# Hybrid decoder layer: products on half of TensorE's array padded to the whole or put in pairs, attention values two blocks at a time

## The chip, the cores and the metric

The kernel runs on one core of a Trainium2 chip. The metric is device time in microseconds for one execution. A core has TensorE (matmuls, into PSUM), VectorE (DVE), ScalarE (ACT), GpSimd (POOL) and SyncE (SP), whose queue issues the DMAs. Each engine works through its own instructions in order and waits for others by semaphores.

## The reference, cut to what matters

One layer with two branches, for 1024 prompt tokens and 64 sample tokens (8 sequences of 8), model width 1024, all in fp32:

```python
proj = rmsnorm(h, norm_mix) @ w_in          # 7440 columns, cut into the parts below
# branch A: gated delta rule, 8 heads of 128, chunks; state S per head and sequence
v_new = u_c - w_c @ S
o_c   = (q_c * exp(g)) @ S + (q k^T * decay) @ v_new
S     = S * exp(g_last) + (k_c * exp(g_last - g)).T @ v_new
# branch B: sliding-window attention, 16 query heads of 64 over 4 key heads, window 128, ALiBi, sinks
p = softmax([s, sink]);  o = p @ v          # the sample tokens see 128 cached keys and their own 8
h = h + (sigmoid(ga) * o_a + sigmoid(gb) * o_b) @ w_out
h = h + relu(rmsnorm(h) @ w_up)**2 @ w_down
h = h + sigmoid(rmsnorm(h) @ w_ple_gate) * (p_l @ w_ple_proj)
```

Outputs are the new hidden rows and the caches: last rows before the convolution, delta-rule states, keys and values of the window.

## The kernel before

Activations lie feature-major: 128 features on the partitions, 1088 tokens (1024 prompt, 64 sample) in the free dimension. Every large product is a "gemm": a weight tile of 128 output features is loaded (512 KB), split into a high and a low part (ScalarE copies to `wh`, GpSimd subtracts into `wl`, both double-buffered), and multiplied against the split activations in three matmuls per contraction tile (lines 165 to 167), over token chunks of 384, 384 and 320 columns. After each group of three matmuls, `part` pops one closure from the list `side`; that is how the small work of attention and of the delta rule is put between the gemm matmuls on TensorE's queue. The small products use plain fp32, which TensorE runs as two passes.

The stages, by the time in the profiled execution:
- Up to 54 us: input norms and the projection of the per-layer embedding.
- 54 to 217 us, keys: for each of 8 heads a gemm tile, the convolution, then `key_rows` and `key_products`, which form k k^T per chunk of 128 tokens (line 587) and for the 64 sample tokens a 64-column product (line 599).
- 217 to 435 us: the triangular solves on VectorE (lines 657, 658), in parallel with gemm tiles for the attention's queries, keys and values. `swa_keys` loads the keys of a key head from DRAM into the buffer `kraw` of its own pool and splits them into `khi` and `klo`; `swa_queries` does so for queries, with one difference per half on GpSimd (line 892).
- Up to 640 us, attention: 8 gemm tiles (gates) with 192 side steps. `attend` runs over n = 0 to 65, three steps for each n: `scores(n)` (lines 921, 922, then VectorE adds the bias and takes the maximum, ScalarE the exponential, line 931), `spread(n-1)` (transposes of the weights, line 944, and one ScalarE copy to `pTs`, 2 buffers), `values(n-2)` (line 966: for two halves of the window and two heads e a product on 64 columns, written to partitions 64e to 64e+63 of `psn`). In every sixth step from the 45th on `swa_sample` advances, in three steps for each of 8 sequences: scores, transposes, and the values (lines 1041, 1042), which for each key head take one product of 128 rows (the cached values `cv`) and one of 64 rows (the new values `vss`), all to the same 64 columns.
- 640 to 1196 us, heads: `gdn_head` for each of 8 heads does four gemm tiles (q, v, z, gate) with the chunk scan (`scan_steps`, lines 1247 to 1270) and the sample's part (`sample_steps`) as side steps. Before them come the products of line 1126 and, for the 64 sample tokens, line 1130. `sample_steps` forms a residual `rs` (64 rows), solves it (line 1216), forms its contribution to the output (line 1227), and updates the 8 states in two blocks of 4 sequences: the new values are multiplied by a mask that keeps the rows of these four (`vm`, line 1223), and a product on 64 rows and 512 columns follows (line 1232). At the next head's start `close` transposes the outputs, the sample's on 64 rows (line 1295).
- From 1196 us: output projection, MLP and embedding gate, nearly all gemm.

The order of instructions on each engine is made by the framework's scheduler from the program's order and its own time model; the times above are the chip's.

Of the kernel before, what the change touches and what calls it, by code (L numbers as in the profile page):

```python
# [9 lines left out]
F32 = mybir.dt.float32  # L10
# [7 lines left out]
P = 128  # L18
# [5 lines left out]
H = 8  # L24
# [5 lines left out]
NUP = 32  # L30

# [7 lines left out]
def hybrid_layer(ctx: ExitStack, tc: tile.TileContext, d):  # L39
# [313 lines left out]
    def small(name, n, parts=P, **kw):  # L353
        return lp.tile([parts, n], F32, name=name, tag=name, **kw)
# [6 lines left out]
    xts = small("xts", H * NS, NS)  # L361
# [4 lines left out]
    vss = mp.tile([NS, 4, 64], F32, name="vss")  # L366
# [182 lines left out]
    def key_rows(h, kT):  # L549

        dma(kTd[h], kT)
        E = kp.tile([P, T], F32, name="E", tag="E", bufs=1)
        dma(E[:, :NP], gcd[h * 8 : h * 8 + 8].rearrange("c p -> (c p)")[None, :].broadcast_to([P, NP]))
        dma(E[:, NP:T], gcsd[h : h + 1].broadcast_to([P, NS]))
# [54 lines left out]

    todo = []  # L610
    for h in range(H + 2):
        st = conv_steps(8 + h, kp, lambda: kp.tile([P, T], F32, name="kT", tag="kT")) if h < H else feature_steps()
# [89 lines left out]
    def solve_sample():  # L702
# [31 lines left out]
        for b in range(NB):  # L734
            ts(out=xts.rearrange("p (h b i) -> p h b i", b=NB, i=8)[:, :, b], in0=xe, scalar1=bsel[:, b : b + 1],
               scalar2=None, op0=ALU.mult)
# [36 lines left out]
    def swa_v(i, vf):  # L773

        yield
        vt = qp.tile([P, 9, P], F32, name="vt", tag="vt", bufs=1)
        tok_major(vf, vf[:, NP:T], vt, 1.0)
        dma(d["o_vp"][:, i], vt[:, 7])
        dma(d["o_vs"][:, i], vt[:NS, 8])
        dma(vtd[i], vt[:, 0:8].rearrange("p c f -> p (c f)"))  # L780
        nc.gpsimd.tensor_copy(vss[:, 2 * i : 2 * i + 2].rearrange("p k d -> p (k d)"), vt[:NS, 8])
# [154 lines left out]
    def spread(n):  # L936
# [8 lines left out]
        pT = sp.tile([P, 2, 2, P], F32, name="pTs", tag="pTs")  # L945
# [39 lines left out]
    def attend():  # L985

        for n in range(64 + 2):
# [6 lines left out]
            if 0 <= n - 2 < 64:  # L994
                values(n - 2)
            yield

    def swa_sample():
# [6 lines left out]
        ts(out=nskc, in0=skc, scalar1=-1.0, scalar2=None, op0=ALU.mult)  # L1005
        for b in range(NB):
# [10 lines left out]
            pr = sl.tile([P, P + NS], F32, name="prs", tag="prs", bufs=1)  # L1017
            st = sl.tile([P, 8], F32, name="sts", tag="sts", bufs=2)
            nm, su, es = st[:, 0:1], st[:, 1:2], st[:, 2:3]
            rb_ = rqs[:, b : b + 1]  # L1020
            stt(out=pr[:, :P], in0=S[:, :P], scalar=rb_, in1=tc_, op0=ALU.mult, op1=ALU.add)
            stt(out=pr[:, P:], in0=S[:, P : P + NS], scalar=rb_, in1=tn_[:, b], op0=ALU.mult, op1=ALU.add)
            nc.vector.tensor_reduce(out=nm, in_=pr, axis=AX.X, op=ALU.max)
            stt(out=nm, in0=nm, scalar=-1.0, in1=nskc, op0=ALU.mult, op1=ALU.min)
            act(pr, pr, AF.Exp, bias=nm, accum_out=su)
# [3 lines left out]
            ts(out=pr, in0=pr, scalar1=es, scalar2=None, op0=ALU.mult)  # L1029
            yield  # L1030
            pt = pst()
            nc.tensor.transpose(pt[:, 0:P], pr[:, :P], ident)
            nc.tensor.transpose(pt[:NS, P : 2 * P], pr[:, P:], ident)
            pT = sl.tile([P, 2 * P], F32, name="pTsb", tag="pTsb", bufs=1)
            act(pT[:, :P], pt[:, :P], AF.Copy)
            act(pT[:NS, P:], pt[:NS, P : 2 * P], AF.Copy)
# [6 lines left out]
            pv = po[:64, :P].rearrange("p (j e t) -> p e j t", e=2, t=8)  # L1043
            for e in range(2):
                act(obs[e * 64 : e * 64 + 64, :, b * 8 : b * 8 + 8], pv[:, e], AF.Copy)
# [39 lines left out]
    gp = pool(actx, "gp")  # L1085
    mixd = dr.tile([KT, P, T], F32, name="mixd")

    def gdn_head(h, prev):
# [3 lines left out]
        kT = G("gkT", [P, T], 2)  # L1092
        kt = G("gkt", [P, 8, P])
        kts = G("gkts", [NS, P])
        rg = G("rg", [P, T], 2)
# [3 lines left out]
        dma(rg, Ed[h])  # L1099
        dma(kT, kTd[h])  # L1100
# [29 lines left out]
        mm(ps[:NS, :NS], kT[:, NP:T], q[:, NP:T], start=True, stop=True)  # L1130
# [61 lines left out]
        ot = G("ot", [P, 9, P])  # L1192

# [8 lines left out]
        def sample_steps():  # L1202
# [8 lines left out]
            r = gp.tile([NS, P], F32, name="rs", tag="rs")  # L1211
            stt(out=r, in0=pk[:NS, :P], scalar=nres[:, h : h + 1], in1=vt[:NS, 8], op0=ALU.mult, op1=ALU.add)
# [3 lines left out]
            mm(ps[:NS, :P], xts[:, h * NS : h * NS + NS], r, start=True, stop=True)  # L1216
            vn = gp.tile([NS, P], F32, name="vns", tag="vns")
            act(vn, ps[:NS, :P], AF.Copy)
            vms = []
            for hf in range(2):  # L1220
                vm = gp.tile([NS, 4, P], F32, name="vm", tag="vm")
                bs = slice(hf * 4, hf * 4 + 4)
                tt(vm, vn[:, None, :].broadcast_to([NS, 4, P]), bsel[:, bs][:, :, None].broadcast_to([NS, 4, P]), ALU.mult)
                yield
                if hf == 0:
                    ps = pst()
                    mm(ps[:NS, :P], qk[:NS, NP:T], vn, start=True, stop=True)
                    tt(ot[:NS, 8], ps[:NS, :P], ot[:NS, 8], ALU.add)
                    out_norm(ps[:NS, :P], NS, 8)
                    yield  # L1230
                ps = pst()
                mm(ps, kts, vm.rearrange("p b n -> p (b n)"), start=True, stop=True)  # L1232
                sb = s0[:, bs].rearrange("p b n -> p (b n)")
                tt(sb, sb, ps, ALU.add)
# [51 lines left out]
        def close():  # L1286
            for hf in range(2):
# [246 lines left out]
```

## Time and profile before

| | |
|---|---|
| median of 3 runs | 2181.7 us (2180.86 to 2184.86) |
| profiled execution | 2175.17 us, span 2173.4 us |
| TensorE matmuls busy | 2111.1 us (97%) |
| VectorE, ScalarE, GpSimd busy | 1081.9, 796.6, 706.7 us |
| mean granted TensorE clock | 0.986 |
| DMA | 196.62 MB, 27.6% of 16 engines' span |

"Busy" is the time in which at least one instruction of an engine is under way; the ends of matmuls are modelled, and matmuls overlap, so the distance between the starts of two matmuls says more of TensorE's pace than their lengths. The profiled execution is one of the kernel's executions, taken with the hardware profiler.

### The profile page before, as it was taken

The page shows a single profiled execution, that of the slowest core. Times are in us where ns is not written, and L with a number is a line of the kernel's source. Part 1 is how long each engine was busy: PE and PEld are TensorE (multiplying, and loading weights), DVE is VectorE, ACT ScalarE, POOL GpSimd, SP SyncE. Part 2 cuts the span into 40 slices and gives each one's busy share as a digit, 9 for nine tenths or more (in the row PEclk, how much of TensorE's full clock was granted, in tenths as well). Part 3 has the DMA queues.
Part 4 walks back from the last instruction along what each step waited for, and adds up shares of the span by engine and source line. Part 5 has one row for each costly group of instructions (what it writes and reads, how often), then busy time and mean ns, then how long its engine had stood idle before and what let it go on. Part 6 is the DMA issues. An engine that isn't in the chain of part 4 may idle for free.

```text
span 2173.4 us, 33492 instructions
## 1 busy us (share of the span) xinstructions
PE 2111.1 (97%) x13485; PEld 2010.5 (93%) x13485; DVE 1081.9 (50%) x1724; ACT 796.6 (37%) x1951; POOL 706.7 (33%) x616
## 2 busy tenths in 40 slices
PE   7999998899999999999999999999999999999999
PEld 6899998777889999999998999999999999999999
DVE  6454599776644555455545543233332323333654
ACT  6576432576643443343335223122121212212321
POOL 4333355333234444544445321212121221212121
PEclk9999999999999999999999999999999999999999
DMA  6465343432143133222332221111111111111132
GB/s 245 140 202 186 106 154 104 128 118 91 64 139 101 64 98 121 94 73 86 111 112 78 88 89 40 39 49 42 46 49 39 49 39 49 47 42 49 39 125 80
DMA packets 89575, 196.62 MB, mean 90 GB/s; under 512 B 34124, under 2 KB 45260, under 8 KB 89292
## 3 DMA queue, kind: packets, MB, share of 16 engines
q1 hardware_dynamic: 89420, 194.48, 27.6%
q8 instruction: 106, 1.74, 0.3%
q14 instruction: 49, 0.40, 0.1%
HBM read 145.61 MB, written 50.78 MB: 90 GB/s over the span
## 4 chain that ended last, share of the span: by engine, by line
PE 80%; DVE 10%; ACT 4%; issue 3%; DMA 1%; POOL 1%; SPq 0%; DVEq 0%; ACTq 0%; POOLq 0%
PE ps L165 23%; PE ps L167 22%; PE ps L166 22%; DVE fs L657 3%; DVE LT L658 2%; PE psn L966 1%; PE pst L944 1%; PE psc L1252 1%; PE pst L1232 1%; PE psc L921 1%; ACT pst L568 1%; PE psc L1247 1%; PE psc L922 1%; PE pst L1126 1%; PE psn L1264 1%
## 5 line engine op out<-in xcount | busy, mean ns | idle before, releaser
L134 POOL TENSOR_TENSOR wl<-wr,wh 128x1024 fp32r<-128x1024 f32 x140 | 343.7, 2455 | 903.8 <-ACT wh L133 903.8
L165 PE MATMUL ps<-xh,wh 128*128 128x384 f32 (+1 forms) x1800 | 626.5, 348 | 3.0 <-ACT qf L349 1.6
L166 PE MATMUL ps<-xl,wh 128*128 128x384 f32 (+1 forms) x1800 | 597.6, 332 | 0.0
L167 PE MATMUL ps<-xh,wl 128*128 128x384 f32 (+1 forms) x1800 | 594.5, 330 | 0.0
L165 PEld LDWEIGHTS ps<-xh,wh 128*128 128x128 f32 x1800 | 341.2, 190 | 26.2 <-issue 21.0
L133 ACT ACTIVATE wh<-wr 128x1024 fp32r<-128x1024 f32 x143 | 150.8, 1054 | 526.1 <-PE ps L166 444.2
L166 PEld LDWEIGHTS ps<-xl,wh 128*128 128x128 f32 x1800 | 341.7, 190 | 1.6 <-issue 0.7
L167 PEld LDWEIGHTS ps<-xh,wl 128*128 128x128 f32 x1800 | 340.6, 189 | 1.9 <-issue 0.9
L165 PE MATMUL ps<-uh,wh 128*128 128x384 f32 (+1 forms) x768 | 250.7, 326 | 1.2 <-DVE h L1403 1.2
L167 PE MATMUL ps<-uh,wl 128*128 128x384 f32 (+1 forms) x768 | 250.9, 327 | 0.0
L166 PE MATMUL ps<-ul,wh 128*128 128x384 f32 (+1 forms) x768 | 250.6, 326 | 0.0
L1403 DVE TENSOR_TENSOR h<-h,ps 128x384 f32<-128x384 f32 (+1 forms) x192 | 100.6, 531 | 226.3 <-PE ps L167 226.3
L166 PE MATMUL ps<-pl,wh 128*128 128x384 f32 (+1 forms) x600 | 197.5, 329 | 0.0
L165 PE MATMUL ps<-ph,wh 128*128 128x384 f32 (+1 forms) x600 | 197.4, 329 | 0.0
L167 PE MATMUL ps<-ph,wl 128*128 128x384 f32 (+1 forms) x600 | 197.0, 329 | 0.0
L1389 DVE TENSOR_TENSOR ul<-us,uh 128x384 fp32r<-128x384 f32 (+1 forms) x96 | 98.0, 1022 | 115.3 <-ACT uh L1388 115.3
L165 PEld LDWEIGHTS ps<-uh,wh 128*128 128x128 f32 x768 | 144.1, 188 | 2.0 <-DVE h L1403 2.0
L167 PEld LDWEIGHTS ps<-uh,wl 128*128 128x128 f32 x768 | 144.1, 188 | 0.0
L166 PEld LDWEIGHTS ps<-ul,wh 128*128 128x128 f32 x768 | 144.1, 188 | 0.0
L508 DVE SCALAR_TENSOR_TENSOR cacc<-raw,cw,cacc 128x1112 f32<-128x1112 f32 x72 | 109.5, 1521 | 62.0 <-ACT cacc L506 56.7
L1387 ACT ACTIVATE us<-ut 128x384 f32<-128x384 f32 (+1 forms) x96 | 48.2, 502 | 197.6 <-DVE ut L1386 196.1
L1386 DVE SCALAR_TENSOR_TENSOR ut<-ps,rb 128x384 f32<-128x384 f32 (+1 forms) x96 | 51.3, 535 | 138.2 <-PE ps L167 138.2
(407 smaller groups left out, 3472.1 us busy)
## 6 DMA issues: line engine op xcount, KB each, us to landing
wr<-win SPq DMA_DIRECT2D x60, 512.0 KB
wr<-wup SPq DMA_DIRECT2D x32, 512.0 KB
wr<-wdn SPq DMA_DIRECT2D x32, 512.0 KB
ppd<-ppo SPq DMA_DIRECT2D x8, 544.0 KB
kTd<-kT SPq DMA_DIRECT2D x8, 544.0 KB
Ed<-E SPq DMA_DIRECT2D x8, 544.0 KB
rg<-Ed SPq DMA_DIRECT2D x8, 544.0 KB
gkT<-kTd SPq DMA_DIRECT2D x8, 544.0 KB
```

What stands on the lines that cost most here:

```text
L133: act(hv, rv, AF.Copy)
L134: (nc.gpsimd if i > 1 else nc.vector).tensor_tensor(lv, rv, hv.bitcast(F32), ALU.subtract)
L165: mm(ps[:M, :w], a, h[:, c0 : c0 + w], start=(k == 0), stop=False)
L166: mm(ps[:M, :w], a, l[:, c0 : c0 + w], start=False, stop=False)
L167: mm(ps[:M, :w], b, h[:, c0 : c0 + w], start=False, stop=(k == n - 1))
L508: stt(out=cc, in0=raw[:, j : j + CONVW], scalar=cw[:, f, j : j + 1], in1=cc, op0=ALU.mult, op1=ALU.add)
L657: tt(tmp, X[:, j : j + 1, j + 1 :].broadcast_to(sh), X[:, 0:j, j : j + 1].broadcast_to(sh), ALU.mult)
L658: tt(X[:, 0:j, j + 1 :], X[:, 0:j, j + 1 :], tmp, ALU.add)
L1386: stt(out=t, in0=ps[:, :w], scalar=0.0, in1=rb2[:, c0 : c0 + w], op0=ALU.max, op1=ALU.mult)
L1387: act(s, t, AF.Square)
L1389: tt(lo[:, c0 : c0 + w], s, hi[:, c0 : c0 + w].bitcast(F32), ALU.subtract)
L1403: tt(hc, hc, ps[:, :w], ALU.add)
```

## The change

What it does:
- Attention: `values` runs for two blocks in a row in every second step, with four buffers of `pTs`. `kraw` is gone; the keys are loaded into `klo` itself and replaced there by the difference.
- Sample attention: the new values and the transposed weights get rows of zeros up to 128, and the output of key heads of odd number goes to partitions 64 to 127.
- Sample products of the delta rule: the stationary operand is widened from 64 to 72 columns (`MS`) and, where the contraction ran over 64 rows, `rs`, `vns`, `xts` and the decay matrix get zero rows; the transpose of line 1295 takes 128 rows. GpSimd writes the zeros.
- State update: one mask multiplication; each half of the sequences uses the 32 rows that belong to it, both products in one step.

```diff
+MS = 72
...
-    xts = small("xts", H * NS, NS)
+    xts = small("xts", H * NS + MS - NS)
+    nc.gpsimd.memset(xts, 0.0)
...
-    vss = mp.tile([NS, 4, 64], F32, name="vss")
+    vss = mp.tile([P, 4, 64], F32, name="vss")
+    nc.gpsimd.memset(vss[NS:P], 0.0)
...
+        nc.gpsimd.memset(E[NS:P, NP:T], 0.0)
...
-        mm(ps[:NS, :NS], kT[:, NP:T], kT[:, NP:T], start=True, stop=True)
+        mm(ps[:MS, :NS], kT[:, NP : NP + MS], kT[:, NP:T], start=True, stop=True)
...
-        raw = ep.tile([P, NP], F32, name="kraw", tag="kraw", bufs=1)
...
+        raw = lo.bitcast(F32)
...
-        pT = sp.tile([P, 2, 2, P], F32, name="pTs", tag="pTs")
+        pT = sp.tile([P, 2, 2, P], F32, name="pTs", tag="pTs", bufs=4)
...
-            if 0 <= n - 2 < 64:
+            if n % 2 and n > 1:
+                values(n - 3)
                 values(n - 2)
...
-            for kv in range(4):
-                o = slice(kv * 32, kv * 32 + 32)
-                mm(po[:64, o], cv[:, kv], pT[:, o], start=True, stop=False)
-                mm(po[:64, o], vss[:, kv], pT[:NS, P + kv * 32 : P + kv * 32 + 32], start=False, stop=True)
...
+            for i in range(2):
+                for c, v in enumerate((cv, vss)):
+                    for e in range(2):
+                        kv = 2 * i + e
+                        mm(po[e * 64 : e * 64 + 64, i * 32 : i * 32 + 32], v[:, kv], pT[:, c * P + kv * 32 : c * P + kv * 32 + 32],
+                           start=(c == 0), stop=(c == 1))
...
-        kT = G("gkT", [P, T], 2)
+        kT = G("gkT", [P, NP + MS], 2)
+        nc.gpsimd.memset(kT[:, T:], 0.0)
...
-        mm(ps[:NS, :NS], kT[:, NP:T], q[:, NP:T], start=True, stop=True)
+        mm(ps[:MS, :NS], kT[:, NP : NP + MS], q[:, NP:T], start=True, stop=True)
...
-            r = gp.tile([NS, P], F32, name="rs", tag="rs")
+            r = gp.tile([P, P], F32, name="rs", tag="rs")
+            nc.gpsimd.memset(r[NS:P], 0.0)
...
-            mm(ps[:NS, :P], xts[:, h * NS : h * NS + NS], r, start=True, stop=True)
+            mm(ps[:MS, :P], xts[:, h * NS : h * NS + MS], r, start=True, stop=True)
+            vn = gp.tile([P, P], F32, name="vns", tag="vns")
+            nc.gpsimd.memset(vn[NS:P], 0.0)
...
+            tt(vm, vn[:NS, None, :].broadcast_to(sh4), bsel4[:, :, None].broadcast_to(sh4), ALU.mult)
+            yield
+            ps = pst()
+            mm(ps[:MS, :P], qk[:, NP : NP + MS], vn, start=True, stop=True)
...
+            pss = [pst() for _ in range(2)]
+            for hf, ps in enumerate(pss):
+                o = slice(hf * 32, hf * 32 + 32)
+                mm(ps, kts[o], vm[o].rearrange("p b n -> p (b n)"), start=True, stop=True)
...
-                    nc.tensor.transpose(pt[:, :NS], ot[:NS, 8], ident[:NS, :NS])
+                    nc.tensor.transpose(pt[:, :P], ot[:, 8], ident)
```

## Rows read from the trace of the kernel before

**Rows 1.** The page, busy us (share of the span) xinstructions.
```profile
PE 2111.1 (97%) x13485; PEld 2010.5 (93%) x13485; DVE 1081.9 (50%) x1724; ACT 796.6 (37%) x1951; POOL 706.7 (33%) x616
```
**Rows 2.** Stretches: length, busy us of PE, PEld, DVE, ACT, POOL, PEclk, DMA.
```profile
366.00:435.00 69.00, 54.66 (x346) 47.92 (x346) 54.61 (x98) 32.63 (x77) 20.65 (x10) 0.89 0.38 119
435.00:640.00 205.00, 199.83 (x1592) 166.81 (x1589) 130.14 (x303) 126.78 (x377) 62.54 (x39) 0.99 0.31 97
640.00:1196.00 556.00, 545.86 (x3609) 502.97 (x3608) 284.51 (x455) 217.47 (x640) 267.80 (x351) 0.99 0.30 96
```
**Rows 3.** Chain of waits from 435 to 640 us, shares by line.
```profile
by line: PE ps L165 14.3%; PE psn L966 13.9%; PE pst L944 10.8%; PE ps L166 10.5%; PE ps L167 10.3%; PE psc L921 5.3%; PE psc L922 5.1%; DMA gkt<-ktd 4.0%; PE pst L1041 3.6%; PE pst L1042 3.6%; ACT pr L931 2.2%; DVE nm L929 2.1%; DVE pr L92
```
**Rows 4.** TensorE in order of time (start us, us, instruction): whole and half product.
```profile
811.76 0.34 PE L165 MATMUL ps<-xh,wh 128*128 128x384 f32 x1
811.94 0.40 PE L1252 MATMUL psc<-r,xt 128*128 128x128 f32 x2
812.09 0.42 PE L166 MATMUL ps<-xl,wh 128*128 128x384 f32 x1
812.35 0.34 PE L167 MATMUL ps<-xh,wl 128*128 128x384 f32 x1
812.61 0.43 PE L1216 MATMUL pst<-rs,xts 64*64 64x128 f32 x2
812.97 0.44 PE L165 MATMUL ps<-xh,wh 128*128 128x384 f32 x1
813.25 0.34 PE L166 MATMUL ps<-xl,wh 128*128 128x384 f32 x1
```
**Rows 5.** TensorE in order of time, one block of the state update.
```profile
683.29 0.42 PE L167 MATMUL ps<-xh,wl 128*128 128x384 f32 x1
683.64 1.12 PE L1232 MATMUL pst<-vm,gkts 64*128 64x512 f32 x2
684.69 0.44 PE L165 MATMUL ps<-xh,wh 128*128 128x384 f32 x1
```
**Rows 6.** TensorE in order of time, one block of attention values.
```profile
515.82 0.31 PE L167 MATMUL ps<-xh,wl 128*128 128x320 f32 x1
516.06 0.66 PE L966 MATMUL psn<-pTs,vt 128*64 128x128 f32 x8
516.64 0.42 PE L165 MATMUL ps<-xh,wh 128*128 128x320 f32 x1
516.90 0.31 PE L166 MATMUL ps<-xl,wh 128*128 128x320 f32 x1
```
**Rows 7.** TensorE in order of time, first and last of a sample block's values.
```profile
603.88 0.30 PE L1041 MATMUL pst<-pTsb,cv 128*64 128x32 f32 x2
...
605.72 0.41 PE L165 MATMUL ps<-xh,wh 128*128 128x320 f32 x1
```
**Rows 8.** TensorE in order of time, a 64-column product behind whole ones.
```profile
1001.02 1.95 PE L1126 MATMUL pst<-q,gkT 128*128 128x128 f32 x16
1002.89 0.33 PE L1130 MATMUL pst<-q,gkT 128*64 128x64 f32 x2
1003.15 0.66 PE L1139 MATMUL psn<-cst,q 128*128 128x128 f32 x4
```
**Rows 9.** Waits from 435 to 640 us: total us, times, longest.
```profile
PEld pst L944 <- ACT pr L931: 5.3, 13, 0.8
```
**Rows 10.** GpSimd and VectorE in order of time, second key head's operands.
```profile
417.31 5.69 POOL L892 TENSOR_TENSOR qst<-qraw,qst 64x1024 fp32r<-64x1024 f32 x2 [4.42 <-ACT qst L891]
419.38 1.42 DVE L879 TENSOR_TENSOR klo<-kraw,khi 128x1024 fp32r<-128x1024 f32 x1 [5.69 <-ACT khi L878]
```
**Rows 11.** GpSimd and TensorE in order of time, between two sample products.
```profile
812.21 2.37 POOL L134 TENSOR_TENSOR wl<-wr,wh 128x1024 fp32r<-128x1024 f32 x1 [2.39 <-ACT wh L133]
...
815.92 0.61 POOL L1200 TENSOR_SCALAR ot<-ot,sso 128x128 f32<-128x128 f32 x1
...
817.14 0.43 PE L1227 MATMUL pst<-vns,rg 64*64 64x128 f32 x2
```

More of the change, by code (lines that the diff above doesn't have):

```diff
@@ L549, in key_rows @@
     def key_rows(h, kT):
-        dma(kTd[h], kT)
+        dma(kTd[h], kT[:, :T])
         E = kp.tile([P, T], F32, name="E", tag="E", bufs=1)
         dma(E[:, :NP], gcd[h * 8 : h * 8 + 8].rearrange("c p -> (c p)")[None, :].broadcast_to([P, NP]))
-        dma(E[:, NP:T], gcsd[h : h + 1].broadcast_to([P, NS]))
+        dma(E[:NS, NP:T], gcsd[h : h + 1].broadcast_to([NS, NS]))
         tt(E[:, :NP].rearrange("p (c n) -> p c n", n=P), E[:, :NP].rearrange("p (c n) -> p c n", n=P),
@@ L608, in feature_steps, with key_tile @@
         yield from tile_steps(xs, evac_to(t))
+    def key_tile():
+        kT = kp.tile([P, NP + MS], F32, name="kT", tag="kT")
+        nc.gpsimd.memset(kT[:, T:], 0.0)
+        return kT
     todo = []
     for h in range(H + 2):
-        st = conv_steps(8 + h, kp, lambda: kp.tile([P, T], F32, name="kT", tag="kT")) if h < H else feature_steps()
+        st = conv_steps(8 + h, kp, key_tile) if h < H else feature_steps()
         next(st)
@@ L734, in solve_sample @@
         for b in range(NB):
-            ts(out=xts.rearrange("p (h b i) -> p h b i", b=NB, i=8)[:, :, b], in0=xe, scalar1=bsel[:, b : b + 1],
+            ts(out=xts[:NS, : H * NS].rearrange("p (h b i) -> p h b i", b=NB, i=8)[:, :, b], in0=xe, scalar1=bsel[:, b : b + 1],
                scalar2=None, op0=ALU.mult)
@@ L780, in swa_v @@
         dma(vtd[i], vt[:, 0:8].rearrange("p c f -> p (c f)"))
-        nc.gpsimd.tensor_copy(vss[:, 2 * i : 2 * i + 2].rearrange("p k d -> p (k d)"), vt[:NS, 8])
+        nc.gpsimd.tensor_copy(vss[:NS, 2 * i : 2 * i + 2].rearrange("p k d -> p (k d)"), vt[:NS, 8])
     def swa_q(j):
@@ L1005, in swa_sample @@
         ts(out=nskc, in0=skc, scalar1=-1.0, scalar2=None, op0=ALU.mult)
+        pr = sl.tile([P, 2 * P], F32, name="prs", bufs=1)
+        nc.gpsimd.memset(pr[:, P + NS :], 0.0)
         for b in range(NB):
@@ L1020, in swa_sample @@
             rb_ = rqs[:, b : b + 1]
+            pk = pr[:, : P + NS]
             stt(out=pr[:, :P], in0=S[:, :P], scalar=rb_, in1=tc_, op0=ALU.mult, op1=ALU.add)
-            stt(out=pr[:, P:], in0=S[:, P : P + NS], scalar=rb_, in1=tn_[:, b], op0=ALU.mult, op1=ALU.add)
-            nc.vector.tensor_reduce(out=nm, in_=pr, axis=AX.X, op=ALU.max)
+            stt(out=pr[:, P : P + NS], in0=S[:, P : P + NS], scalar=rb_, in1=tn_[:, b], op0=ALU.mult, op1=ALU.add)
+            nc.vector.tensor_reduce(out=nm, in_=pk, axis=AX.X, op=ALU.max)
             stt(out=nm, in0=nm, scalar=-1.0, in1=nskc, op0=ALU.mult, op1=ALU.min)
-            act(pr, pr, AF.Exp, bias=nm, accum_out=su)
+            act(pk, pk, AF.Exp, bias=nm, accum_out=su)
             act(es, skc, AF.Exp, bias=nm)
@@ L1028, in swa_sample @@
             nc.vector.reciprocal(es, es)
-            ts(out=pr, in0=pr, scalar1=es, scalar2=None, op0=ALU.mult)
+            ts(out=pk, in0=pk, scalar1=es, scalar2=None, op0=ALU.mult)
             yield
             pt = pst()
-            nc.tensor.transpose(pt[:, 0:P], pr[:, :P], ident)
-            nc.tensor.transpose(pt[:NS, P : 2 * P], pr[:, P:], ident)
+            for c in range(2):
+                nc.tensor.transpose(pt[:, c * P : c * P + P], pr[:, c * P : c * P + P], ident)
             pT = sl.tile([P, 2 * P], F32, name="pTsb", tag="pTsb", bufs=1)
-            act(pT[:, :P], pt[:, :P], AF.Copy)
-            act(pT[:NS, P:], pt[:NS, P : 2 * P], AF.Copy)
+            act(pT, pt[:, : 2 * P], AF.Copy)
             yield
             po = pst()
-            for kv in range(4):
-                o = slice(kv * 32, kv * 32 + 32)
-                mm(po[:64, o], cv[:, kv], pT[:, o], start=True, stop=False)
-                mm(po[:64, o], vss[:, kv], pT[:NS, P + kv * 32 : P + kv * 32 + 32], start=False, stop=True)
-            pv = po[:64, :P].rearrange("p (j e t) -> p e j t", e=2, t=8)
-            for e in range(2):
-                act(obs[e * 64 : e * 64 + 64, :, b * 8 : b * 8 + 8], pv[:, e], AF.Copy)
+            for i in range(2):
[4 more added lines that the diff above has]
+                           start=(c == 0), stop=(c == 1))
+            for f in range(2):
+                pv = po[f * 64 : f * 64 + 64, :64].rearrange("p (i g e t) -> p e i g t", i=2, e=2, t=8)
+                ov = obs.rearrange("p (i f g) s -> p f i g s", f=2, g=2)[:, f]
+                for e in range(2):
+                    act(ov[e * 64 : e * 64 + 64, :, :, b * 8 : b * 8 + 8], pv[:, e], AF.Copy)
             yield
@@ L1085, in hybrid_layer @@
     gp = pool(actx, "gp")
+    bsel4 = gp.tile([NS, 4], F32, name="bsel4")
+    tt(bsel4, bsel[:, 0:4], bsel[:, 4:8], ALU.add)
     mixd = dr.tile([KT, P, T], F32, name="mixd")
@@ L1091, in gdn_head @@
         hs = slice(h * 8, h * 8 + 8)
-        kT = G("gkT", [P, T], 2)
+        kT = G("gkT", [P, NP + MS], 2)
+        nc.gpsimd.memset(kT[:, T:], 0.0)
         kt = G("gkt", [P, 8, P])
         kts = G("gkts", [NS, P])
-        rg = G("rg", [P, T], 2)
+        rg = G("rg", [P, NP + MS], 2)
+        nc.gpsimd.memset(rg[:, T:], 0.0)
         xt = G("xt", [P, 8, P], 2)
@@ L1098, in gdn_head @@
         x11, bl = xb[0:64], xb[64:128]
-        dma(rg, Ed[h])
-        dma(kT, kTd[h])
+        dma(rg[:, :T], Ed[h])
+        dma(kT[:, :T], kTd[h])
         for hf in range(2):
@@ L1192, in gdn_head @@
         ot = G("ot", [P, 9, P])
+        nc.gpsimd.memset(ot[NS:P, 8], 0.0)
         def out_norm(junk, w, c):
@@ L1215, in sample_steps @@
             ps = pst()
-            mm(ps[:NS, :P], xts[:, h * NS : h * NS + NS], r, start=True, stop=True)
[L1217 to L1233, printed above, removed]
+            mm(ps[:MS, :P], xts[:, h * NS : h * NS + MS], r, start=True, stop=True)
+            vn = gp.tile([P, P], F32, name="vns", tag="vns")
+            nc.gpsimd.memset(vn[NS:P], 0.0)
+            act(vn[:NS], ps[:NS, :P], AF.Copy)
+            vm = gp.tile([NS, 4, P], F32, name="vm", tag="vm")
+            sh4 = [NS, 4, P]
+            tt(vm, vn[:NS, None, :].broadcast_to(sh4), bsel4[:, :, None].broadcast_to(sh4), ALU.mult)
+            yield
+            ps = pst()
+            mm(ps[:MS, :P], qk[:, NP : NP + MS], vn, start=True, stop=True)
+            tt(ot[:NS, 8], ps[:NS, :P], ot[:NS, 8], ALU.add)
+            out_norm(ps[:NS, :P], NS, 8)
+            yield
+            pss = [pst() for _ in range(2)]
+            for hf, ps in enumerate(pss):
+                o = slice(hf * 32, hf * 32 + 32)
+                mm(ps, kts[o], vm[o].rearrange("p b n -> p (b n)"), start=True, stop=True)
+            for hf, ps in enumerate(pss):
+                sb = s0[:, hf * 4 : hf * 4 + 4].rearrange("p b n -> p (b n)")
                 tt(sb, sb, ps, ALU.add)
```

3 lines of the change are left out of this document (1 added, 2 removed).

## Prediction, made before the change was run

> **What bounds the kernel now.** I read the page's busy times first: TensorE's matmuls fill 97% of the span [rows 1]. A busy matmul row alone proves nothing, since matmuls overlap, so the second view is the busy time by stretch [rows 2]. From 366 to 435 us TensorE works 54.66 of 69 us and its clock falls to 0.89: it waits for the triangular solve on VectorE, and what is saved there is waited away. From 435 to 640 us (attention) and from 640 to 1196 us (the eight heads of the delta rule) it works 97% and 98%, at a granted clock of 0.99, which is the 2.4 GHz level nearly all the time. The third view, the chain of waits over the attention stretch, runs through TensorE's lines almost alone; the exponentials (ACT L931) hold 2.2% of it [rows 3]. So in both stretches a nanosecond taken from TensorE's queue is one taken from the time, until another engine is late.
>
> The fourth view, TensorE's instructions in order of time, says what the touched products cost. I count from the last gemm matmul before a product to the second one after it, less the regular distances of two gemm matmuls (0.18 us at 384 columns, 0.15 at 320), because the gap behind a product is long too. An fp32 product shows as two passes.
> - Whole array, 128 columns (L1252): 811.76 to 812.35 is 0.59, less 0.36: 0.23 us [rows 4].
> - The same on 64 rows and 64 columns (L1216): 812.35 to 813.25 is 0.90, less 0.36: 0.54 us [rows 4]. The half product is the dearer one by 0.31: it starts 0.26 after its predecessor instead of 0.18, and the gemm after it starts late and is followed late. Entering and leaving the half form is what costs.
>
> **The change part by part.** The sum is made against the profiled execution, 2175.2 us.
> - *Sample products of a head made whole* (L1216, L1227): two per head, 8 heads, 16 x 0.31 = 5.0 us. No row shows 72 columns; the bounds are the half form (gain 0) and the whole one (5.0). 72 don't fit into a half of 64, so I take the whole.
> - *Transpose of 64 rows made whole* (L1295): once per head, no row for a whole one alone; by the same entry and exit 0 to 0.31, I take 0.28: 2.2 us.
> - *64-column products behind whole ones* (L1130, L599): 16 of these. Sixteen whole passes and the entry take 1.87 us, 0.11 each and some 0.11 for the entry; the two half passes then hold 0.26 instead of 0.22 [rows 8], and the exit comes on top. Between 0.1 and 0.31 each, I take 0.22: 3.5 us.
> - *State update* (L1232): before, two blocks per head, each of two passes: 683.29 to 684.69 is 1.40, plus 0.10 late behind it (as in [rows 4]), less 0.18: 1.32 us each [rows 5]. Half of each block's rows are zeros. After, one block with two products on 32 rows each, in different row strips and different PSUM banks. If they run side by side it costs about one block: gain 1.32 x 8 = 10.6 us. If one after another, only one entry and exit go: 0.27 x 8 = 2.2 us. No row shows row strips; the nearest is the attention values on column halves: eight passes from 516.06 to 516.64 are 0.073 us each [rows 6], where whole passes of the same width take 0.11 [rows 8], so two halves do run together. I take 10.6.
>  On this the Trainium skill ("TensorE: Matmul & The Clock Gate", Part 3) says that matmuls in distinct row groups run concurrently, their starts some 4 ns apart; by it the gain is the upper end, and no row here tests it for rows.
> - *Values two blocks at a time* (L966): one block of eight passes costs 515.82 to 516.90, 1.08 less 0.30: 0.78 us [rows 6]. Eight more behind it, in the same form, are four pairs at 0.11: 0.44. Each merge saves 0.34, and there are 32 merges. Eight of them lie before 435 us, where TensorE waits anyway: worth nothing. The other 24 offer 8.1 us. But the values of an even block now come later, so the step without them brings the next transpose (L944) up to 0.78 us nearer to its scores, and TensorE already waits there for the exponentials, 5.3 us in 13 of the steps after 435 us [rows 9]; the step with sixteen passes has room to spare. Between a gain of 8.1 and a loss of 24 x 0.78 - 8.1 = 10.6. By the 13 of 48 steps that have no slack and the others that have some I take half of the gain: 4.0 us.
> - *Sample values* (L1041, L1042): sixteen passes alternate between 128 rows and 64 rows, 603.88 to 605.72, 1.84 us, once per block, eight blocks [rows 7]. After, all have 128 rows and go in eight pairs of column halves. If pairs don't overlap, 16 x 0.11: gain 0.1. If they overlap fully and short columns are cheaper still (0.06 a pair, half of 0.11): gain 1.36. The pairs of [rows 6] speak for pairs at about 0.105: 0.84, gain 1.0, 8.0 us in all; I take 7.0, as TensorE reaches the next transposes earlier. Two copies of the transposed weights on ScalarE become one and two of the output become four; ScalarE works 126.78 of 205 us there [rows 2], so I cost it at nothing.
> - *Keys read into their low part* (L877, buffer "kraw" gone): the loads for the first two key heads can no longer be issued ahead; they wait for the buffer of "klo", that is for the end of the solve's memory, on SP's queue behind the loads of values and masks. The first use is hidden by VectorE, still busy with the solve. The second: the difference ran at 419.38 to 420.80, and GpSimd's query differences, which TensorE needs too, end at 417.31 + 5.69 = 423.00 [rows 10]. That covers 2.2 us of the load. Bounds 0 and 3 us for each of the two; I take 0.7 in all.
> - *Zeros on GpSimd*: some nine small memsets per head. Two stand before a product in the same step: the rows 64 to 127 of "rs" and "vns". Behind the first sample product (812.61 [rows 4]) GpSimd's queue holds a weight difference from 812.21 and an output norm that ends at 815.92 + 0.61 = 816.53; the second product, which needs the zeros of "vns", starts at 817.14 [rows 11]. GpSimd is busy 267.80 of 556 us [rows 2]. I take 0.5 us in all.
> - One mask multiplication less per head on VectorE: not on the path.
>
> Sum: 5.0 + 2.2 + 3.5 + 10.6 + 4.0 + 7.0 - 0.7 - 0.5 = 31.1 us. 2175.2 - 31.1 = 2144.1; the median of the runs lies 6.5 us above the profiled execution, so 2150.6: forecast **2151 us**.
>
> **A rule against it.** The 0.54 against 0.23 us of [rows 4] is for one lone product. The Trainium skill ("TensorEngine Tiling (Array Packing)", "When to Use Tiling") advises the opposite, row or column tiling wherever a dimension is 64 or less; if padding were no gain, the three padding terms would go. That is the third rival.
>
> **The rivals.**
> 1. *The two row strips run one after another.* For: no row shows it. Against: the column pairs. 10.6 - 2.2 = 8.4 us less: 2159.
> 2. *Attention becomes bound by the exponentials.* Each of 24 shortened steps waits its full 0.78 us: 18.7 us lost instead of 4.1, so 14.6 less: 2166. For: 13 waits already; against: they are short, 0.8 us at most [rows 9].
> 3. *Padding buys nothing*, because 72 columns or zeros make these products no cheaper: 5.0 + 2.2 + 3.5 = 10.7 less: 2162. Against: [rows 4].
> 4. *The late key loads are exposed in full*, 6 us: 2156.
> 5. *Slower: TensorE waits for the zeros.* If TensorE stood still while each "vns" memset waits behind a weight difference and a norm (812.21 to 816.53, 4.3 us) and each "rs" memset behind a weight difference (2.4) [rows 11], that is 8 x 6.7 = 54 us: 2205. It decides from 31.1 / 8 = 3.9 us of waiting per head. Against: half of GpSimd's time in this stretch is free.
> 6. *Several of 1 to 3 together*: all three take 33.7 us and leave 2185, no change.
>
> **How the numbers follow.** Forecast 0.46, rival 1 0.18, rival 2 0.15, rival 3 0.04, rival 4 0.05, rival 5 0.06, rival 6 0.06. Faster by over 0.2% (4.4 us, about what a measurement of this kernel can tell from no change): the forecast and rivals 1 to 4, 0.88; within 0.2%: rival 6, 0.06; slower: rival 5, 0.06. The forecast's own range is 2142 to 2160 (the bounds of the sample values and of half the values). For 8 in 10 the range takes in rivals 1 to 4 and, below, the case that all of the 8.1 us and of the sample values' 10.9 come through: 2138 to 2172.
>
> **What would show it right or wrong.** After: the L1216 and L1227 products cost 0.23 us as L1252 does, or still 0.54 (rival 3); one block of L1232's four passes near 1.1 us long, or near 2.1 (rival 1); sixteen values passes in about 1.0 us and half as many blocks; the idle time of L944 behind ACT L931 well over 8 us (rival 2); TensorE idle behind a memset (rival 5). The stretch from 435 to 640 us shortens by some 11 us, that of the heads by some 20. The forecast is wrong if the heads' stretch shortens by less than 10.

## The result, and the profile after

The changed kernel takes 2146.5 us (median of 4 runs, 2144.4 to 2160.1), beside 2181.3 of the kernel before (4 runs): a ratio of 0.987, 95% interval 0.983 to 0.990. The profiled executions are 2145.3 and 2175.2 us.

These times hold two things. The granted clock, as a mean over a run, went from 0.979 to 0.991 in the 133 runs of this study, and within one kernel a run is 1.59 us shorter for each 0.001 of it (one slope fitted through the runs of all kernels). Below, "at 0.985" means that each run was moved along this slope before the mean was taken. A single run then scatters by 2.1 us, so the standard errors are 2.1 over the root of the number of runs. At 0.985 the kernel before takes 2177.5 ± 0.3 us (the 49 runs beside the experiments; the means of the three chips that they ran on lie within 0.5 us) and the changed one 2151.8 ± 1.0: **the change is worth 25.7 ± 1.1 us**. Of the other 9.1 us between the medians, 5.3 are the clock of the changed kernel's runs (2151.8 less 2146.5). The remaining 3.8 lie in the four runs of the kernel before, whose clocks are not all on record; that these are clock as well is not shown.

The page of the changed kernel (busy us, share of the span, instructions) and its stretches (length, busy us of PE, PEld, DVE, ACT and POOL, clock, DMA); the heads' stretch begins and ends where it does in [rows 2], by instruction:
```profile
PE 2072.6 (97%) x13485; PEld 1994.1 (93%) x13485; DVE 1082.6 (51%) x1717; ACT 798.1 (37%) x1959; POOL 715.1 (33%) x675
```
```profile
435.00:640.00 205.00, 192.48 (x1614) 165.05 (x1612) 136.43 (x310) 133.14 (x391) 68.63 (x51) 0.98 0.35 111
636.00:1172.00 536.00, 523.78 (x3609) 496.95 (x3607) 282.74 (x446) 216.71 (x640) 274.85 (x384) 1.00 0.31 99
```
Against [rows 1] TensorE has as many instructions and is busy for 38.5 us less, some 5 us of it by the higher clock (0.989 beside 0.986, by the slope above). Against [rows 2] the heads' stretch is 20 us shorter, 536 for 556; about 3 of these are clock, which stood at 1.2 GHz (granted 0.50) from 648.8 to 655.6 us before and nowhere in this stretch after. From the first score to the first product of the heads (L1126, now L1147) 265.6 us became 256.9, though the mean clock there fell from 0.97 to 0.96. The attention stretch now leaves TensorE idle for 12.5 of its 205 us instead of 5.2: part of the gain there became waiting.

The chain of waits over the attention stretch, shares by line:
```profile
by line: PE ps L166 12.0%; PE psn L975 11.7%; PE ps L167 10.0%; PE ps L168 9.9%; PE pst L953 8.9%; DVE nm L938 7.5%; DVE pr L934 5.6%; ACT pr L940 5.4%; PE psc L930 4.8%; DVE nm L937 4.5%; PE psc L931 3.9%; DMA rd<-dend 2.0%; issue 1.8%; PE
```
In [rows 3] the exponentials and the maxima ahead of them held some 2% each; now the softmax (L934, L937, L938, L940) holds 23%.

TensorE in order of time (start us, us, instruction), the touched blocks: the sample values (before: [rows 7]), the values [rows 6], a sample product of a head (L1216 in [rows 4]) and the state update [rows 5].
```profile
493.51 0.31 PE L1056 MATMUL pst<-pTsb,cv 128*64 128x32 f32 x4
493.65 0.29 PE L1056 MATMUL pst<-pTsb,vss 128*64 128x32 f32 x4
493.76 0.29 PE L1056 MATMUL pst<-pTsb,cv 128*64 128x32 f32 x4
493.88 0.29 PE L1056 MATMUL pst<-pTsb,vss 128*64 128x32 f32 x4
494.10 0.45 PE L166 MATMUL ps<-xh,wh 128*128 128x384 f32 x1
...
518.77 0.31 PE L168 MATMUL ps<-xh,wl 128*128 128x320 f32 x1
519.01 1.09 PE L975 MATMUL psn<-pTs,vt 128*64 128x128 f32 x16
520.03 0.44 PE L166 MATMUL ps<-xh,wh 128*128 128x384 f32 x1
520.31 0.34 PE L167 MATMUL ps<-xl,wh 128*128 128x384 f32 x1
...
800.15 0.33 PE L168 MATMUL ps<-xh,wl 128*128 128x384 f32 x1
800.32 0.38 PE L1240 MATMUL pst<-rs,xts 128*72 128x128 f32 x2
800.46 0.43 PE L166 MATMUL ps<-xh,wh 128*128 128x384 f32 x1
800.72 0.33 PE L167 MATMUL ps<-xl,wh 128*128 128x384 f32 x1
...
808.12 0.34 PE L168 MATMUL ps<-xh,wl 128*128 128x384 f32 x1
808.39 1.13 PE L1257 MATMUL pst<-vm,gkts 32*128 32x512 f32 x4
809.44 0.44 PE L166 MATMUL ps<-xh,wh 128*128 128x384 f32 x1
809.73 0.34 PE L167 MATMUL ps<-xl,wh 128*128 128x384 f32 x1
```
Counted as in the prediction (last gemm matmul before to the second one after, less 0.36 or 0.33): the sample product costs 0.21 us for 0.54; one block of state update 809.73 - 808.12 - 0.36 = 1.25 for two of 1.32; sixteen values passes 520.31 - 518.77 - 0.33 = 1.21 for twice 0.78; sample values from first pass to the next gemm 0.59 for 1.84.

What a head takes is read from one instruction that recurs in every head. First before, then after: the first such product of the third and of the last head, five heads apart.
```profile
788.40 0.27 PE L1126 MATMUL pst<-q,gkT 128*128 128x128 f32 x1
...
1142.97 0.38 PE L1126 MATMUL pst<-q,gkT 128*128 128x128 f32 x2
```
```profile
776.39 0.27 PE L1147 MATMUL pst<-q,gkT 128*128 128x128 f32 x1
...
1120.79 0.27 PE L1147 MATMUL pst<-q,gkT 128*128 128x128 f32 x1
```
354.57 / 5 = 70.9 us and 344.40 / 5 = 68.9 us, both at a granted clock of 1.00. A head gained 2.0 us, eight of them 16, where the cheaper blocks offer 2.4 a head (added up below, under *Heads*).

### The profile page after: what moved, and what is told of

It is laid out like the page before. It is cut to its first block, busy times and chain, and to the rows that moved or that the text cites. A ratio compares the mean times of both kernels' runs of the same rounds, so it can differ in the third digit from the quotient of the medians.

```text
span 2143.5 us, 33612 instructions
## 1 busy us (share of the span) xinstructions
PE 2072.6 (97%) x13485; PEld 1994.1 (93%) x13485; DVE 1082.6 (51%) x1717; ACT 798.1 (37%) x1959; POOL 715.1 (33%) x675
## 4 chain that ended last, share of the span: by engine, by line
PE 79%; DVE 10%; ACT 5%; issue 3%; POOL 1%; DMA 1%; SPq 0%; ACTq 0%; DVEq 0%; POOLq 0%
PE ps L166 23%; PE ps L168 22%; PE ps L167 22%; DVE fs L666 2%; DVE LT L667 2%; PE psn L975 1%; PE pst L953 1%; ACT wh L134 1%; DVE nm L938 1%; PE psc L1278 1%; ACT pst L572 1%; ACT pr L940 1%; PE psc L1273 1%; PE pst L1147 1%; PE psc L930 1%
```

## The experiments

Each kernel ran beside the kernel before on the same chip. The changed kernel itself ran only four times, beside none of these; e6, which differs from it in the zeros alone, lies within 0.8 us of it. At 0.985, with standard errors:

| run | what | runs | us at 0.985 | against |
|---|---|---|---|---|
| e1_state64 | state products on 64 rows each | 6 | 2158.5 ± 0.9 | changed +6.7 ± 1.4 |
| e2_single | values one block at a time | 6 | 2158.0 ± 0.9 | changed +6.2 ± 1.4 |
| e3_lag | spread two blocks behind | 6 | 2143.2 ± 0.9 | changed -8.6 ± 1.4 |
| e4_single_lag | both of these | 6 | 2153.4 ± 0.9 | e3 +10.2 ± 1.2 |
| e5_before_klo | before, keys into klo | 10 | 2182.2 ± 0.7 | before +4.7 ± 0.7 |
| e6_zeros_once | zeros written once | 4 | 2151.0 ± 1.0 | changed -0.8 ± 1.5 |
| e7_ms64 | 64 columns again | 6 | 2158.6 ± 0.9 | changed +6.8 ± 1.4 |
| e8_before_sample | before, sample values | 10 | 2170.3 ± 0.7 | before -7.2 ± 0.7 |
| e9_keys_tg | first keys into a gate buffer | 6 | 2155.8 ± 0.9 | changed +4.0 ± 1.4 |
| e10_lag_keys_tg | e3 and e9 | 4 | 2143.8 ± 1.0 | e3 +0.6 ± 1.4 |
| e11_lag_keys_tg_pr4 | e10, four pr and three pTs | 4 | 2143.3 ± 1.0 | e10 -0.5 ± 1.5 |
| e12_before_lag | before, spread two behind | 12 | 2179.6 ± 0.6 | before +2.1 ± 0.7 |

**e1_state64: do the row strips run side by side?**
```diff
-                o = slice(hf * 32, hf * 32 + 32)
-                mm(ps, kts[o], vm[o].rearrange("p b n -> p (b n)"), start=True, stop=True)
+                mm(ps, kts, vm.rearrange("p b n -> p (b n)"), start=True, stop=True)
```


> The changed kernel, with both products of the sample states' update on all 64 rows instead of on 32 rows each (the mask still one multiplication a head; each half of the states also gets the other half's rows, so the states that it writes differ). Theory: the gain of this part came from the two 32-row products running at once (one block of 1.26 us in the changed kernel's trace, where the two of the kernel before took 1.30 us each). Then a head pays a second 1.3 us again: 8 x 1.3 = 10.7 us slower than the changed kernel, 2155 to 2158 us, and the block reads about 2.6 us. Rival: the two strips run one after the other or no faster than the whole, and the gain came from the one mask in place of two and the shorter chain: then within 1.5 us of the changed kernel (2145 to 2148 us), block about 1.3 us.

The block of e1, TensorE in order of time, and the same block in the last head:
```profile
812.99 0.34 PE L168 MATMUL ps<-xh,wl 128*128 128x384 f32 x1
813.25 1.98 PE L1256 MATMUL pst<-vm,gkts 64*128 64x512 f32 x4
815.16 0.44 PE L166 MATMUL ps<-xh,wh 128*128 128x384 f32 x1
815.45 0.34 PE L167 MATMUL ps<-xl,wh 128*128 128x384 f32 x1
...
1161.77 0.69 PE L1256 MATMUL pst<-vm,gkts 64*128 64x512 f32 x1
```
They run side by side: the same four passes of 512 columns take 815.45 - 812.99 - 0.36 = 2.10 us on 64 rows and 1.25 on strips of 32. Rival 1 of the prediction falls. But the price I expected was too high. I had reckoned two lone blocks of 1.3 us, and two products that follow each other in one block share an entry and an exit, so what concurrency alone is worth is 0.85 us a head. A head is (1161.77 - 813.25) / 5 = 69.7 us, 0.8 more than the 68.9 of the changed kernel: all of it is seen, 6.6 us in eight heads.

**e7_ms64: which direction makes a half product dear?**
```diff
-MS = 72
+MS = 64
```


> The changed kernel with the rows still padded to 128, but the outputs of the padded products at 64 columns again, as in the kernel before. Theory: a product that is half in either direction pays the price of entering and leaving the form: the two products of a head go from 0.23 us back to 0.4 to 0.56, those of the keys and of the queries back to what they were: 16 x (0.17 to 0.33) + 8 x 0.28 + 8 x 0.17 = 6.3 to 8.9 us of TensorE's time, of which the waits in a head hide up to half: 4 to 8 us slower than the changed kernel, a head 69.4 to 69.7 us for 68.9. Rival: only the rows (the weights' partitions) cost: the two products of a head stay at 0.23 us, and only keys and queries return, 3.6 us or less, a head at most 69.1 us.

The sample product of e7, TensorE in order of time, and its start in the last head:
```profile
806.01 0.33 PE L168 MATMUL ps<-xh,wl 128*128 128x384 f32 x1
806.27 0.43 PE L1237 MATMUL pst<-rs,xts 128*64 128x128 f32 x2
806.63 0.44 PE L166 MATMUL ps<-xh,wh 128*128 128x384 f32 x1
...
1153.14 0.32 PE L1237 MATMUL pst<-rs,xts 128*64 128x128 f32 x1
```
On all 128 rows and 64 columns it starts 0.26 us after its predecessor and is followed 0.36 later, as in [rows 4] on 64 rows: half the columns alone bring back the whole price. Half the rows alone are dear as well: the transpose of 64 rows and 128 columns (L1295) took 0.39 us in the kernel before, on 128 rows (L1321) 0.14, counted in the same way over eight heads. The kernel is 6.8 us slower, within what was expected. A head is (1153.14 - 806.27) / 5 = 69.4 us, half a microsecond more, though TensorE's blocks are dearer by 0.8 (0.33 for each of two, 0.17 behind L1147). What took the rest shows in the waits of the heads' stretch (total us, times, longest), in the kernel before, the changed one and e7:
```profile
PE psc L1247 <- DVE S L1262: 3.9, 8, 0.5
```
```profile
PE psc L1273 <- DVE S L1288: 6.5, 8, 0.8
```
```profile
PE psc L1270 <- DVE S L1285: 3.9, 8, 0.5
```
Once in every head the scan waits for its state S, and with cheap sample products it waits 0.33 us longer. VectorE in the changed kernel at that place, in order of time:
```profile
801.04 1.89 DVE L1246 TENSOR_TENSOR vm<-vns,bsel 64x512 f32<-64x512 f32 x1
802.85 0.33 DVE L1288 SCALAR_TENSOR_TENSOR S<-S,egl,psc 128x128 f32<-128x128 f32 x1
```
TensorE's next scan product starts at 803.24. The mask multiplication holds VectorE from 801.04 until S, queued behind it, starts at 802.85. It begins when the padded product before it (L1240, at 800.32) has been copied, at 801.01, and VectorE's gate multiplication ahead of it has ended, at 801.06, so each saving ahead of it brings the scan to the same queue earlier: 8 x 0.33 = 2.6 us of the heads' gain are waited away there. I had costed the masks as "not on the path".

**e2_single, e3_lag, e4_single_lag: what are pairs of blocks worth, and what do the exponentials eat?** e3 moves the spread; e2 takes the pairs apart; e4 does both.
```diff
 # e2
-            if n % 2 and n > 1:
-                values(n - 3)
+            if 0 <= n - 2 < 64:
                 values(n - 2)
 # e3
-        for n in range(64 + 2):
+        for n in range(64 + 3):
-            if 0 <= n - 1 < 64:
-                spread(n - 1)
+            if 0 <= n - 2 < 64:
+                spread(n - 2)
-            if n % 2 and n > 1:
+            if n % 2 == 0 and n > 2:
+                values(n - 4)
                 values(n - 3)
-                values(n - 2)
```


> The changed kernel, with the attention values one block at a time again, everything else as changed. Theory: the 24 merges offer 24 x 0.35 = 8.4 us of TensorE's time, and the waits of the transposes for the exponentials eat half: 4 us slower than the changed kernel, 2149 to 2152 us. Rival A: the exponentials set the pace of the attention and the pairs bought nothing: within 1 us of it, 2146 to 2147.5. Rival B: the pairs bought all that they offer: 8 us slower, 2154 to 2156.

> The changed kernel, with the spread (the transposes of the exponentials) two blocks behind the scores instead of one, and the values in pairs one block later too. Theory: the waits of the transposes for the exponentials in the attention (in the changed kernel's trace 12.4 us before weight loads and 6.1 us before transposes, in the kernel before 5.3 us) are a matter of lag and go: 5 to 12 us faster than the changed kernel, 2134 to 2141 us. Rival A: ScalarE and VectorE set the pace between gate products, and the wait moves to the scores' buffers (prs, psc): within 1.5 us, 2145 to 2148. Rival B: the three pr buffers, now held a block longer, make the scores wait and it is slower by 2 to 6 us.

> The changed kernel with the values one block at a time and the spread two blocks behind the scores. With the three others it makes a square of two by two. Theory: without waits for exponentials a merge shows its whole price: this one is 24 x 0.35 = 8.4 us slower than the kernel with pairs and the same lag, and 3 to 5 us faster than single values at a lag of one (the 5.3 us of such waits in the trace of the kernel before). Rival A: exponentials' pace: all four within 2 us. Rival B: lag buys the same with and without pairs, and the pairs' gain is the same 4 us at either lag, so that the half that is missing was never lost to these waits.

e2 by itself, 6.2 ± 1.4 us, lies between its theory (4) and its rival B (8) and decides for neither. With the others: pairs are worth 6.2 us with the spread one block behind and 10.2 with it two behind; the extra block of distance is worth 4.6 us without pairs and 8.6 with them. The square has the form that the theory gave it: merging offers 24 x 0.35 = 8.4 us, and perhaps a little more ahead of 435 us, which wasn't tried; at the old distance 4.0 us of it are missing, and the waits for the exponentials show where (each of these differences has an error of 1.2 to 1.8 us, so the 4.0 are some two errors from nothing). The waits of the attention in the changed kernel and in e3 (435 to 640 and 435 to 630 us; before: [rows 9]):
```profile
PE pst L953 <- ACT pr L940: 6.1, 11, 1.9
PEld pst L953 <- ACT pr L940: 12.4, 25, 2.2
```
```profile
PE pst L953 <- ACT pr L940: 2.0, 3, 1.3
PEld pst L953 <- ACT pr L940: 3.1, 5, 1.6
```
5.3 us of waiting before weight loads became 12.4 by the change and 3.1 by the distance. The rivals "exponentials set the pace" and "three pr buffers hold the scores" fall with it. e3's ratio to the kernel before is 0.985 (0.982 to 0.987); it is faster than both kernels.

**e12_before_lag: is the distance a gain without the change?** The kernel before, with the same two edits around spread and with values(n - 3) single.
```diff
-            if 0 <= n - 1 < 64:
-                spread(n - 1)
+            if 0 <= n - 2 < 64:
+                spread(n - 2)
-            if 0 <= n - 2 < 64:
-                values(n - 2)
+            if 0 <= n - 3 < 64:
+                values(n - 3)
```


> The kernel before with the spread two blocks behind the scores and the values three, nothing of the change. Theory: its waits for the exponentials, 5.3 us before weight loads and 2.1 us before transposes, go: 4 to 7 us faster than before at the same clock, as with single values in the changed kernel (4.7 us). Rival: without the change there is nothing to win, within 1.5 us.

It is 2.1 ± 0.7 us slower: the theory misses, and the rival (within 1.5 us) is not excluded. Its waits from 435 to 640 us:
```profile
PE psc L921 <- DVE pr L925: 4.9, 3, 2.1
PEld psc L921 <- DVE pr L925: 5.7, 4, 2.3
PEld psn L966 <- ACT pr L931: 1.0, 4, 0.3
```
The waits of the transposes for the exponentials are gone, and the scores wait for their psc tiles instead, which VectorE has not read yet (in the kernel before no such wait reaches 1 us). In e4, single values at the same distance, the distance pays. The two differ in the four buffers of pTs, the keys and the sample values; which of these turns the sign wasn't tried.

**e8_before_sample: the sample values alone.** Of the diff, the edits of vss and of the loop over b in swa_sample, put into the kernel before:
```diff
+    vss = mp.tile([P, 4, 64], F32, name="vss")
+    nc.gpsimd.memset(vss[NS:P], 0.0)
+        pr = sl.tile([P, 2 * P], F32, name="prs", bufs=1)
+        nc.gpsimd.memset(pr[:, P + NS :], 0.0)
...
```


> The kernel before with one part of the change alone: the values of the samples' attention (padded rows, two key heads beside each other, one copy of the transposes). Theory: eight blocks give 1.0 to 1.25 us each, 8 to 10 us, nearly all of it seen: 6.5 to 9 us faster than before at the same clock, all of it between the first score and the last value. That fits the changed kernel, where at the same clock this stretch is 12.7 us shorter with pairs of blocks and 7.1 us shorter with single ones. Rival: TensorE waits there for the samples' exponentials instead, 2 us or less.

7.2 us, as the theory had it and as the prediction took it (7.0). The blocks are 1.25 us cheaper, 10 us in all; the rest fits new waiting in the same stretch: between 375 and 640 us the waits for the exponentials before the transposes' weight loads grew from 8.2 to 10.9 us.

**e5_before_klo, e9_keys_tg: what does it cost to load the keys into klo?**
```diff
 # e5
-        raw = ep.tile([P, NP], F32, name="kraw", tag="kraw", bufs=1)
+        raw = lo.bitcast(F32)
 # e9
-        raw = lo.bitcast(F32)
+        raw = lo.bitcast(F32) if kv else ep.tile([P, T], F32, name="tg", tag="tg")[:, :NP]
```


> The kernel before with one part of the change alone: the raw keys land in the tile klo instead of kraw. Theory: the stretch from the last key product to the first score, 162.3 us in the profile of before and 163.4 to 164.1 us in the five profiles with the change, grows by the same 1.8 us here, and the later key loads are hidden: at the same granted clock 1 to 2 us slower than before. Rival A (the second-to-last rival of the prediction): each of the four key loads shows, 4 to 8 us slower. Rival B: it costs nothing and the 1.8 us come from another part.

> The changed kernel, with the raw keys of the first key head landing in a buffer of the gate tiles (tg), which exists while the solve runs, instead of in klo, which doesn't; the other three loads stay in klo. Theory: the 4.8 us that the key loads cost at an equal clock (the kernel before with them alone) are the first load's, whose difference of the keys ran at 385.6 us in place of 376.4: 3 to 5 us faster than the changed kernel at the same clock, and the first score's second product no longer waits for klo. Rival: the price lies in all four loads, or in the clock: less than 1.5 us.

e5 is 4.7 us slower than before: the size of rival A, not of the theory, though the trace doesn't show each of the four loads. TensorE's waits at the first score, in the kernel before and then in e5 (from 375 and 380 us on):
```profile
PE psc L921 <- DVE qst L892: 8.2, 1, 8.2
```
```profile
PE psc L921 <- DVE qst L892: 4.3, 1, 4.3
PE psc L922 <- DVE klo L879: 4.3, 1, 4.3
```
The wait for klo is new, but the wait for the queries ahead of it is shorter by nearly as much: 8.6 us in all for 8.2. The tile klo in the changed kernel and in e9, first keys (start of first and last, then who waited):
```profile
L888 DVE TENSOR_TENSOR klo<-klo,khi x4: 1212/1222/1294, 385.6 to 505.4; 128x1024 fp32r<-128x1024 f32 x4
...
PEld psc L931: 4.8, 1
PE psc L931: 4.3, 1
```
```profile
L888 DVE TENSOR_TENSOR klo<-tg,khi x1: 1218/1218/1218, 382.7 to 382.7; 128x1024 fp32r<-128x1024 f32 x1
...
PEld psc L931: 0.8, 1
PE psc L931: 0.4, 1
```
e9 took away nearly all of the only wait of TensorE for klo that is long, and was 4.0 us slower than the changed kernel: neither its theory nor its rival. It is no clean removal, since the raw keys now hold one of the two gate buffers until that difference, which may cost something of its own. By the sums of e5 the price of the key loads isn't in longer waits at the first score. It isn't in waits for the later loads either that the trace names: the second difference, at 419.38 us in [rows 10], runs at 440.79 in the changed kernel, and no wait of TensorE is put down to it. What e5 does show is its chain of waits from 435 to 645 us:
```profile
by line: PE ps L165 13.0%; PE psn L966 12.4%; PE pst L944 10.1%; PE ps L166 9.6%; PE ps L167 9.4%; PE psc L921 5.0%; DVE nm L929 4.6%; PE psc L922 4.4%; DVE pr L925 4.3%; PE pst L1041 3.5%; PE pst L1042 3.5%; ACT pr L931 3.4%; DVE nm L928 2
```
VectorE's maxima hold 4.6% where [rows 3] has 2.1, and the exponentials 3.4 for 2.2: the softmax comes nearer to the path. By which operation of the keys stays open.

**e10_lag_keys_tg, e11_lag_keys_tg_pr4: do the two add up, and do buffers matter?** e10 is e3 and e9 together; e11 adds
```diff
-        pr = sp.tile([P, 2, 2 * P], F32, name="pr", tag="pr", bufs=3)
+        pr = sp.tile([P, 2, 2 * P], F32, name="pr", tag="pr", bufs=4)
-        pT = sp.tile([P, 2, 2, P], F32, name="pTs", tag="pTs", bufs=4)
+        pT = sp.tile([P, 2, 2, P], F32, name="pTs", tag="pTs", bufs=3)
```


> The changed kernel with both: the spread two blocks behind the scores, and the first raw keys in a tg buffer. Theory: 8.6 us (the lag, at an equal clock) and 3 to 5 us add up: 11 to 13.5 us faster than the changed kernel at the same clock, 2138 to 2141 us at 0.985. Rival: both shorten the same start of the attention, and it is no faster than the lag alone (8.6 us).

> The last one with four buffers of pr and three of pTs instead of three and four. Theory: at a lag of two blocks the waits left in the attention (2.0 and 3.1 us for the exponentials, 3.5 us for pTs) are short, and neither count of buffers sets the pace: within 1.5 us of it. Rival: three buffers of pr held the scores back, 2 to 4 us faster; or three of pTs are too few for pairs, 2 to 4 us slower.

Neither adds to the lag: all three lie within 0.6 us of each other at 0.985 (e10's ratio to the kernel before is 0.983, 0.980 to 0.986), as e10's rival had it. With the distance the first keys' place costs 0.6 ± 1.4 us, where without it it cost 4.0 ± 1.4: what e9 disturbs seems to be hidden once the spread is two blocks behind. Whether the 4.7 us of e5 are hidden too wasn't tried. e11 changes both counts of buffers at once, so a gain of one and a loss of the other could cancel in it.

**e6_zeros_once: does TensorE wait for the zeros?** rs, vns and ot became one lasting buffer each, with the memset ahead of the heads.
```diff
-            nc.gpsimd.memset(r[NS:P], 0.0)
-            nc.gpsimd.memset(vn[NS:P], 0.0)
-        nc.gpsimd.memset(ot[NS:P, 8], 0.0)
+    nc.gpsimd.memset(ot0[NS:P, 8], 0.0)
+    nc.gpsimd.memset(rs0[NS:P], 0.0)
+    nc.gpsimd.memset(vn0[NS:P], 0.0)
```


> The changed kernel with the rows of zeros in rs, vns and ot written once ahead of the heads (each is one lasting buffer) instead of in every head. Theory: GpSimd's zeros are off the path: a head stays at 68.9 us and the whole within 1.5 us of the changed kernel at the same clock. Rival (TensorE waits for zeros): a head gets 0.3 to 0.7 us shorter, 2.5 to 5.5 us in all.

It makes no difference: -0.8 ± 1.5 us, and a head stays at 68.9. Rival 5 falls, and so does my 0.5.

## Why the prediction was right, and where not

The forecast of 2151 us and its range held the 2146.5 measured. But its sum was 31.1 us, and at an equal clock the change is worth 25.7. That the number came so close is luck: the clocks of the changed kernel's own runs (three of four at 0.988 or 0.989) hid the difference, and at 0.985, where 2151.8 meets the forecast again, a base 4 us too high (2181.7 for 2177.5) covers a sum 5 us too large. By its steps:

- *The bound* was read rightly: TensorE in attention and heads. The first key products, the heads and the attention all gave.
- *Heads* (5.0 + 2.2 + 10.6 and half of 3.5, 19.6 us): 16. The prices of the blocks were right: 0.33 a product (taken 0.31), 0.25 a transpose (L1321 next to L1295; taken 0.28), 0.17 behind L1147 (taken 0.22), 1.32 for the state update (over all heads two blocks of 1.28 became one of 1.25), of which 0.85 is the strips running at once (e1) and the rest one entry for two: 2.4 a head. The step that failed is "one mask multiplication less ... not on the path": the mask that is left, with S queued behind it, took back 2.6 us.
- *Key products* (the other half of 3.5): 1.1 us; from the first to the last of them 117.4 us became 116.3. Mis-sized: 0.14 a product for 0.22.
- *Values* (4.0): 6.2 by e2. The mechanism was the one described; what the waits take, 4.0 us (10.2 by e3 and e4 less 6.2), was sized as 4.1, right within its error of 1.8, and the offer was the larger by 2.
- *Sample values* (7.0): 7.2 by e8, in part by luck: the blocks offered 10.0 us and not 8.0, and 2.8 were lost and not 1.0.
- *Keys* (-0.7): -4.7 by e5. This is the term that was wrong: I priced the exposure of two loads behind the work that covers them, 2.2 us of slack for the second. The second difference came 21 us later and no wait of TensorE names it, and at the first score e5 waits 0.4 us longer in all, so exposure isn't what the trace shows as the cost. The upper bound of 6 held, so did rival 4 as a price, with another mechanism than the one given.
- *Zeros* (-0.5): none by e6.

16 + 1.1 + 6.2 + 7.2 - 4.7 + 0 = 25.8, beside 25.7 measured. The terms come from different kernels and have errors of up to 1.4 us, so they agree with the whole within some 2 us; the agreement to 0.1 is chance. Open are by which operation the keys cost 4.7 us, and why the longer distance pays only with the change.

Of the rivals, 1 falls by e1, 3 by e7, 6 with both, 5 by e6. Rival 2 was there at less than its price, 4.0 us for 14.6. On row groups (the Trainium skill, "TensorE: Matmul & The Clock Gate", Part 3) the trace agrees, 1.25 against 2.10 us for four passes. On tiling wherever a dimension is 64 or less (the Trainium skill, "TensorEngine Tiling (Array Packing)", "When to Use Tiling") it differs for lone products: 0.54 us on the half array and 0.21 on the whole, and e7's 6.8 us decide for padding.

## What to carry to other kernels

A product that stands alone among whole ones is priced by the change of form, not by its size: pad it, or put all half products of a step next to each other and let them share one entry. Before a gain on the busiest engine is counted, look at what comes next on its path in the same step: here TensorE met the softmax with waits of 0.5 us on average (12.4 us in 25) and one VectorE multiplication with 0.3 us more in each head, and a longer distance between producer and consumer gave back more than the change lost there. And a buffer dropped to save memory needs a price of its own, measured alone.

## What the runs showed of the hardware

- Half the columns alone (128 rows, 64 columns, e7) cost a lone fp32 product 0.55 us, as much as half of both (0.54, L1216 before); 72 columns cost 0.21, no more than a full 128 (0.23, [rows 4]).
- Half the rows alone (64 rows, 128 columns) are dear too: one pass of the transpose cost 0.39 us before, 0.14 on 128 rows after.
- Two products of 512 columns on 32 rows each, in different row strips and PSUM banks, take 1.25 us together (changed kernel); on 64 rows one after another, 2.10 (e1).
- Between the runs of one kernel the mean granted clock changed by up to 0.010, and with it the time by some 16 us, over half of what this change is worth. Comparing two medians of 4 runs overstated the gain by 9 us.
